# First block's mixers: mLSTM ended by pairs of heads, output projection begun with seven of eight blocks, keys' norm by logarithm and exponential

## The chip, the cores and the metric

One core of a Trainium2 chip runs the whole program. The metric is the device time in microseconds of one execution. The kernel before takes 3124.77 us, the median of three runs (3122.93 to 3128.39).

## The reference, cut to what matters

A sequence of 512 tokens of width 1024 goes through two blocks. The change lies in the first block, which computes

```python
u = x @ w_in                                   # four mixers side by side, 256 columns out of each
y = concat(ssd(u0), rwkv(u1), gla(u2), mlstm(u3))      # 512 x 1024
x = layer_norm(alpha * x + y @ w_out)          # the output projection
logits = x @ router_w + router_b               # top 4 of 32 experts
x = layer_norm(alpha * x + moe(x) + ...)
```

Two details of the mixers are touched. RWKV divides its keys by their norm, per head of 64 channels: `kk = kk / max(norm(kk), 1e-12)`. The mLSTM has four heads of 64 channels, each with its own scores (512 x 512, causal), its own denominator `max(|den|, exp(-m))` and, after the output gate `sigmoid(og)`, its own group norm with centring. So the heads are independent of each other to the very end, where the output projection sums over all 1024 channels of the four mixers.

## The kernel before, in words

**The first block's mixers** are `block1_mix`. Channels lie on partitions where it suits (tiles of 128 x 512 tokens) and tokens lie on partitions elsewhere (tiles of 128 tokens x 4 chunks x 256 channels). Inputs and weights are split into a rounded half and a rest (`split`, lines 437 and 438), and a product is three matmuls (lines 449 to 451 and 466 to 468). `fproj` makes 128 channels on partitions, `tproj` is a generator that makes 256 channels with tokens on partitions, one chunk of 128 tokens at each `next`.

**The order of the work** is set by the framework's scheduler: the code is traced once, each engine then takes, among the instructions that are ready, the one that stands first in the program, and the result is one fixed order for each engine and each DMA queue. Buffers come from tagged pools: a tag has so many slots, and a tile takes a slot when its first instruction is issued. PSUM has eight banks; in `block1_mix` they belong to the pools `ps` (2, taken by `psb`), `pi` (3, the RWKV solves) and `pp` (3, the projections). After `block1_mix` the pool `psum` takes all eight anew, from the bottom: tag `gu` four (over both banks of `ps` and two of `pi`), `tr` two, `py` two. A tile of a new pool waits for the old tiles that lay in its place, and for no others.

**RWKV's keys** (`rwkv_prep`, lines 841 to 904, once for each half j of 128 channels): the keys are scaled (850), squared on ScalarE (851), summed per head by a matmul with a block matrix (853), and then come `Sqrt` on ScalarE (854), a maximum with 1e-12 (855) and a reciprocal (856) on VectorE, and the product (857). Beside it the decay's running sum is made and three exponentials are taken of it (869, 871, 872). The product goes to 875 and to GpSimd (877); the chain runs on over 878 to 885, after which TensorE makes the bonus (888) and the transposes (893, 899).

**The mLSTM** (`mlstm`, lines 729 to 789) comes last. For each head h and each key chunk si it makes decay weights on VectorE (752), takes their exponential on ScalarE (754), masks the diagonal on GpSimd (755), makes the scores on TensorE (757) and multiplies on VectorE (758); then ten products with the values (763) and a copy out of PSUM to `nd` on ScalarE (765). Between the heads `next(gate)` puts one chunk of the output gate's projection `mog`, whose `tanh` goes to `og` (744). After the four heads the activation table for logarithm and exponential is loaded (768), the projection's pools are closed, `out_begin` opens the tiles `mix` (the 1024 mixed channels, split) and `wo` (the split output weights) over the place of the closed pools, and the end follows for all four heads at once on 128 x 1024 elements: denominator (773 to 777), quotient (779), gate (781) and `post_norm` (566 to 572, with `fast_rsqrt`, lines 1083 to 1085). Then the pieces of `finish` of SSD, GLA and RWKV transpose their two blocks of 128 channels into `mix` (580, 583 to 587), the eight pieces of `w_out` are loaded and split (`out_piece`: 802, 804, 805), and the mLSTM's own two blocks are transposed. `fin` holds the four mixers' pieces in the order SSD, GLA, RWKV, mLSTM.

**The output projection** is in `block1_ffn`: for each of four token chunks t and two halves n of the columns it takes one bank `gu` and adds 8 blocks x 3 matmuls (`mm3`, lines 1148 to 1150), 192 in all. Then come the residual (1283), the layer norm (`row_norm`), the transposes (1297), the router (1301), the top four and the tables for the experts. The first expert starts with the gather of its rows (1428) and their transposes (1230). Then 32 experts run, one after the other, on weights that are streamed through a ring of buffers (1204) and split on ScalarE and VectorE (1213, 1214).

Of the kernel before, what the change touches and what calls it, by code (L numbers as in the profile page):

```python
# [8 lines left out]
F32 = mybir.dt.float32  # L9
# [364 lines left out]
def block1_mix(k, es_mix):  # L374
# [4 lines left out]
    with ExitStack() as es:  # L379
# [18 lines left out]
        def P(name, j=0):  # L398
            return colp[:, CP[name][0] + j:CP[name][0] + j + 1]
# [155 lines left out]
        def post_norm(y, nh, eps, center, gname, mi, between=None, fast=False):  # L555


            n = 256 // nh
            yv = y.rearrange("p c (h d) -> p (c h) d", h=nh)
            m = NCH * nh  # L560
            sq = wt([128, NCH, 256], "pn_sq")
# [14 lines left out]
            def finish(mix):  # L576
                for j in range(2):
# [4 lines left out]
                    if gname:  # L582
                        ACT.activation(mh, p, AF.Copy, scale=P(gname, j))
                        V.scalar_tensor_tensor(ml, p, P(gname, j), mh.bitcast(F32), op0=OP.mult, op1=OP.subtract)
# [144 lines left out]
        def mlstm():  # L729
# [16 lines left out]
            Wt = {}  # L746
            for h in range(4):
                j, r = h // 2, slice(64 * (h % 2), 64 * (h % 2) + 64)
                for si in range(NCH):
                    n = S - 128 * si  # L750
                    w = wt([128, n], "ml_w")
                    V.tensor_scalar(w, Gb[h][:, 128 * si:], cols[:, si, 64 + h:65 + h], 0.0,
                                    op0=OP.subtract, op1=OP.max)
                    ACT.activation(w, w, AF.Exp, scale=-1.0)
                    G.tensor_mul(w[:, :128], w[:, :128], C("incl"))
                    p = psb([128, n])
                    PE.matmul(p, kq[j][r, 128 * si:128 * si + 128], q[j][r, 128 * si:], start=True, stop=True)
                    V.scalar_tensor_tensor(w, w, 0.125, p, op0=OP.mult, op1=OP.mult)
                    Wt[si] = w
                p = psb([128, NCH, 65])  # L760
                for ti in range(NCH):
                    for si in range(ti + 1):
                        PE.matmul(p[:, ti], Wt[si][:, 128 * (ti - si):128 * (ti - si) + 128],
                                  mv[:, si, h], start=si == 0, stop=si == ti)
# [6 lines left out]
            den = wt([128, NCH, 4], "ml_den")  # L771
            dn = nd[:, :, :, 64]
            V.tensor_scalar(den, dn, -1.0, None, op0=OP.mult)
            V.tensor_max(den, den, dn)
            V.tensor_max(den, den, em)
            V.reciprocal(den, den)
            V.tensor_scalar(den, den, 0.5, None, op0=OP.mult)
            hh = wt([128, NCH, 256], "ml_h")
            V.tensor_mul(hh.rearrange("p c (h d) -> p c h d", h=4), nd[:, :, :, :64],
                         den[:, :, :, None].to_broadcast([128, NCH, 4, 64]))  # L780
            V.scalar_tensor_tensor(hh, og, 1.0, hh, op0=OP.add, op1=OP.mult)
            post_norm(hh, 4, 1e-5, True, "ml_g", 6, fast=True)
# [5 lines left out]
            fin[3](mix)  # L788

# [20 lines left out]
        def rwkv_prep():  # L810
# [34 lines left out]
            for j in range(2):  # L845
# [307 lines left out]
def block1_ffn(k, mix, wo, es_mix, b2):  # L1153
# [5 lines left out]
    with es:  # L1159
# [78 lines left out]
        with tile_pool(tc, name="w1", bufs=1) as w1:  # L1238
# [1312 lines left out]
```

## Time and profile before

| what | us |
|---|---|
| median of three runs | 3124.77 |
| the profiled execution's own time | 3125.81 |
| its span, from first to last instruction | 3124.0 |
| TensorE busy in the span | 2966.2 (95%) |
| VectorE, ScalarE, GpSimd busy | 2037.0, 1491.3, 537.4 |
| end of the mLSTM's last head (copy to `nd`) | 374.1 |
| first matmul of the output projection | 393.3 |
| last matmul of the output projection | 445.9 |
| first transposes of the first expert's rows | 477.2 |

Rows of the trace give the start in us from the span's beginning, the length, the engine, the line, the operation, the tiles written and read with their shapes, and in brackets the idle time before the instruction and what ended it. A merged row (x8) stands for so many instructions in succession. Engines are PE (TensorE), PEld (its weight loads), DVE (VectorE), ACT (ScalarE) and POOL (GpSimd). PEclk is the granted TensorE clock, 1.00 being 2.4 GHz and 0.50 being 1.2 GHz.

### The profile page before, as it was taken

To read this page: it belongs to the slowest core of one execution; us is meant where nothing else is said; L and a number is where in the kernel's file an instruction comes from. 1 tells how busy PE (TensorE), PEld (TensorE's weight loads), DVE (VectorE), ACT (ScalarE), POOL (GpSimd) and SP (SyncE) were. 2 spreads that over 40 slices of the span, in tenths; PEclk is the share of its full clock that TensorE was granted. 3 is DMA by queue.
4 is the path that set the end of the run, shared out by engine and by line. 5 is a ranking of instruction groups with operands and counts; after the bars stand their busy time and mean duration, and the time that the engine had idled before them with its cause. 6 is when DMAs were issued, how large, how long until landed. Compare 5 with 4: busy or idle time off the path is not lost. (4 is left out here: it accounts for less than half of the span.)

```text
span 3124.0 us, 41785 instructions
## 1 busy us (share of the span) xinstructions
PE 2966.2 (95%) x16609; PEld 2386.3 (76%) x16609; DVE 2037.0 (65%) x2862; ACT 1491.3 (48%) x1855; POOL 537.4 (17%) x444
## 2 busy tenths in 40 slices
PE   6899888999999999999999999999999899999997
PEld 4799765666666666666666888999999799888886
DVE  4755767988888888788887756654233846733324
ACT  4412346666666666666665633342222534432222
POOL 1210231101210000121002210320102501320104
PEclk8989989999999999999999989999999989999998
DMA  3201177989999999799996211122222211222221
GB/s 124 75 21 41 61 268 289 357 341 366 366 358 359 361 359 353 290 388 356 360 355 229 73 67 43 55 82 95 95 82 82 93 45 55 82 95 95 95 90 52
DMA packets 106263, 581.87 MB, mean 186 GB/s; under 512 B 13080, under 2 KB 13736, under 8 KB 56048
## 3 DMA queue, kind: packets, MB, share of 16 engines
q1 hardware_dynamic: 95120, 542.17, 44.9%
q0 software_dynamic: 10752, 36.47, 4.8%
q8 instruction: 132, 2.16, 0.3%
q10 hardware_dynamic: 192, 0.52, 0.1%
q14 instruction: 67, 0.55, 0.1%
HBM read 560.17 MB, written 18.94 MB: 185 GB/s over the span
## 5 line engine op out<-in xcount | busy, mean ns | idle before, releaser
L1214 DVE TENSOR_TENSOR wl<-w,wh 128x2048 fp32r<-128x2048 f32 (+1 forms) x367 | 800.8, 2197 | 125.7 <-ACT wh L1213 121.4
L1213 ACT ACTIVATE wh<-w 128x2048 fp32r<-128x2048 f32 (+1 forms) x375 | 668.3, 1810 | 51.4 <-PE gu L1150 34.9
L1816 PE MATMUL gu<-hh,w 128*128 128x264 f32 (+3 forms) x1336 | 419.0, 314 | 10.0 <-ACT hh L2518 10.0
L1817 PE MATMUL gu<-hl,w 128*128 128x264 f32 (+3 forms) x1336 | 415.6, 311 | 3.9 <-DVE hl L2520 3.8
L1818 PE MATMUL gu<-hh,w 128*128 128x264 f32 (+3 forms) x1336 | 413.5, 310 | 0.8 <-DVE w L1142 0.8
L1142 DVE TENSOR_TENSOR w<-w 128x1024 fp32r<-128x1024 f32 (+1 forms) x190 | 237.5, 1250 | 249.2 <-ACT w L1141 248.7
L1148 PE MATMUL gu<-wh,xT 128*96 128x512 f32 x896 | 371.9, 415 | 0.0
L1149 PE MATMUL gu<-wl,xT 128*96 128x512 f32 x896 | 359.4, 401 | 7.4 <-DVE wl L1214 7.2
L1150 PE MATMUL gu<-wh,xT 128*96 128x512 f32 x896 | 351.4, 392 | 0.0
L1141 ACT ACTIVATE w<-w 128x1024 fp32r<-128x1024 f32 (+1 forms) x194 | 201.3, 1038 | 297.7 <-PE gu L2338 89.6
L1816 PEld LDWEIGHTS gu<-hh,w 128*128 128x128 f32 x1336 | 260.0, 195 | 22.4 <-ACT hh L2518 11.6
L1817 PEld LDWEIGHTS gu<-hl,w 128*128 128x128 f32 x1336 | 260.0, 195 | 16.1 <-DVE hl L2520 5.0
L1818 PEld LDWEIGHTS gu<-hh,w 128*128 128x128 f32 x1336 | 260.5, 195 | 11.2 <-DVE w L1142 1.3
L1149 PE MATMUL py<-wl,hT 128*96 128x512 f32 x512 | 211.7, 413 | 1.8 <-DVE wl L1214 0.4
L1149 PEld LDWEIGHTS gu<-wl,xT 128*96 128x96 f32 x896 | 144.1, 161 | 87.1 <-DVE wl L1214 23.2
L1148 PE MATMUL py<-wh,hT 128*96 128x512 f32 x512 | 208.8, 408 | 1.4 <-ACT wh L1213 1.4
L1150 PE MATMUL py<-wh,hT 128*96 128x512 f32 x512 | 202.8, 399 | 0.0
L1148 PEld LDWEIGHTS gu<-wh,xT 128*96 128x96 f32 x896 | 144.4, 161 | 67.3 <-issue 7.4
L1150 PEld LDWEIGHTS gu<-wh,xT 128*96 128x96 f32 x896 | 145.4, 162 | 58.5
L2324 POOL TENSOR_TENSOR al<-fs,ah 128x528 fp32r<-128x528 f32 (+1 forms) x44 | 77.7, 1767 | 595.0 <-ACT ah L2323 595.0
L1428 POOL DMA_INDIRECT xg<-x_d,ix x32 | 72.8, 2275 | 505.5 <-DVE dx L1421 439.4
L1481 POOL DMA_INDIRECT h_d<-y,dx x31 | 60.6, 1955 | 526.2 <-ACT y L1480 496.6
(714 smaller groups left out, 6133.4 us busy)
## 6 DMA issues: line engine op xcount, KB each, us to landing
w<-in_wgu SPq DMA_DIRECT2D x256, 1024.0 KB, 8.4
w<-in_wdn SPq DMA_DIRECT2D x127, 1024.0 KB, 8.3
w<-in_w SPq DMA_DIRECT2D x88, 512.0 KB, 4.2
w<-in_w2f SPq DMA_DIRECT2D x43, 512.0 KB, 4.2
w<-in_w22a SPq DMA_DIRECT2D x32, 512.0 KB, 4.1
w<-in_w1f SPq DMA_DIRECT2D x18, 512.0 KB, 3.3
w<-in_w2o SPq DMA_DIRECT2D x16, 512.0 KB, 4.2
w<-in_w22b SPq DMA_DIRECT2D x16, 384.0 KB, 3.9
```

The source lines that it names most:

```text
L1141: nc.scalar.activation(h, w, AF.Copy)
L1142: (eng or nc.vector).tensor_sub(l, w, h.bitcast(F32))
L1148: PE.matmul(out, a[0], b[0], start=start, stop=False)
L1149: PE.matmul(out, a[0], b[1], start=False, stop=False)
L1150: PE.matmul(out, a[1], b[0], start=False, stop=stop)
L1213: ACT.activation(h[:, j], w[:, j], AF.Copy)
L1214: (early or V).tensor_sub(l[:, j], w[:, j], h[:, j].bitcast(F32))
L1428: gathers.append(G.indirect_dma_start(out=xg, out_offset=None, in_=x1_d, in_offset=bass.IndirectOffsetOnAxis(ap=ix[:, :1], axis=0)))
L1816: PE.matmul(p, w[0][:, kk], x[0][:, kk, c], start=kk == ks[0], stop=False)
L1817: PE.matmul(p, w[0][:, kk], x[1][:, kk, c], start=False, stop=False)
L1818: PE.matmul(p, w[1][:, kk], x[0][:, kk, c], start=False, stop=kk == ks[-1])
L2324: G.tensor_sub(a[1], ss[f], a[0].bitcast(F32))
```

## The change

Three things change, all in the first block.

1. **mLSTM.** The heads' loop becomes `heads(j)` for the pair 2j and 2j + 1, and the end becomes `end(j)` on that pair's 128 channels. The program order is now: heads 0 and 1 with the whole of the gate's projection, the table load, `out_begin`, `end(0)`, the blocks of SSD, GLA and RWKV, the eight pieces of `w_out`, the first pair's block, and only then heads 2 and 3, `end(1)` and the second pair's block. `post_norm` gets the arguments `j0` and `nb` for one block instead of two.
2. **Output projection.** Before the loop over chunks, four banks are begun (t = 0 and 1, n = 0 and 1) with the first seven blocks of `mix`, 21 matmuls each; the loop then adds the eighth block to these and does chunks 2 and 3 as before. The eighth block is the second pair of heads.
3. **Keys' norm.** The maximum is now taken of the sum of squares, straight from PSUM, with 1e-24; then `Ln` and `Exp` with scale -0.5 follow on ScalarE. Square root and reciprocal are gone.

```diff
-            Wt = {}
-            for h in range(4):
-                j, r = h // 2, slice(64 * (h % 2), 64 * (h % 2) + 64)
-                for si in range(NCH):
...
-                ACT.activation(nd[:, :, h], p, AF.Copy)
-                next(gate)
+            def heads(j):
+                for h in range(2 * j, 2 * j + 2):
+                    r = slice(64 * (h % 2), 64 * (h % 2) + 64)
+                    Wt = {}
+                    for si in range(NCH):
...
+                    ACT.activation(nd[:, :, h], p, AF.Copy)
+                    if j == 0:
+                        for _ in range(2):
+                            next(gate, None)
+
+            hh = wt([128, NCH, 256], "ml_h").rearrange("p c d -> p (c d)")
+            den = wt([128, NCH, 4], "ml_den")
+
+            def end(j):
+                hs_ = slice(2 * j, 2 * j + 2)
+                dj = den[:, :, hs_]
+                dn = nd[:, :, hs_, 64]
+                V.tensor_scalar(dj, dn, -1.0, None, op0=OP.mult)
+                V.tensor_max(dj, dj, dn)
+                V.tensor_max(dj, dj, em[:, :, hs_])
+                V.reciprocal(dj, dj)
+                V.tensor_scalar(dj, dj, 0.5, None, op0=OP.mult)
+                y = hh[:, 512 * j:512 * j + 512].rearrange("p (c d) -> p c d", c=NCH)
+                V.tensor_mul(y.rearrange("p c (h d) -> p c h d", h=2), nd[:, :, hs_, :64],
+                             dj[:, :, :, None].to_broadcast([128, NCH, 2, 64]))
+                V.scalar_tensor_tensor(y, og[:, :, 128 * j:128 * j + 128], 1.0, y, op0=OP.add, op1=OP.mult)
+                post_norm(y, 2, 1e-5, True, "ml_g", 6 + j, fast=True, j0=j, nb=1)
+
+            heads(0)
+            for _ in gate:
+                pass
             with tc.issue_after(last[-1].ins):
                 ACT.preload_act_table_set(LN_EXP)
             es2.close()
             out_begin()
...
-            post_norm(hh, 4, 1e-5, True, "ml_g", 6, fast=True)
+            end(0)
             for f in fin[:3]:
                 f(mix)
             for n in range(2):
                 for i in range(4):
                     out_piece(n, i)
             fin[3](mix)
+            heads(1)
+            end(1)
+            fin[4](mix)
...
-                ACT.activation(sq, p, AF.Sqrt)
-                V.tensor_scalar(sq, sq, 1e-12, None, op0=OP.max)
-                V.reciprocal(sq, sq)
+                V.tensor_scalar(sq, p, 1e-24, None, op0=OP.max)
+                ACT.activation(sq, sq, AF.Ln)
+                ACT.activation(sq, sq, AF.Exp, scale=-0.5)
                 V.tensor_mul(kk, kk, sq)
...
+            begun = {}
+            def project(t, n, qs):
+                c = slice(128 * t, 128 * t + 128)
+                if (t, n) not in begun:
+                    begun[t, n] = bank("gu")
+                for q in qs:
+                    mm3(PE, begun[t, n], (mix[0][:, q, c], mix[1][:, q, c]), (wo[n][0][:, q], wo[n][1][:, q]), q == 0, q == 7)
+                return begun[t, n]
+            for n in range(2):
+                for t in range(2):
+                    project(t, n, range(7))
             for t in range(NCH):
                 c = slice(128 * t, 128 * t + 128)
                 for n in range(2):
-                    p = bank("gu")
-                    for q in range(8):
-                        mm3(PE, p, (mix[0][:, q, c], mix[1][:, q, c]), (wo[n][0][:, q], wo[n][1][:, q]), q == 0, q == 7)
+                    p = project(t, n, range(7 if t < 2 else 0, 8))
```

## Rows read from the trace of the kernel before

**Rows 1.** Windows by stage: length; busy PE, PEld, DVE, ACT, POOL; PEclk, DMA, GB/s
```profile
376.80:393.30 16.50, 5.22 (x24) 3.97 (x24) 15.92 (x19) 12.30 (x18) 0.33 (x1) 0.64 0.67 224
393.30:398.60 5.30, 5.26 (x13) 4.17 (x14) 0.00 (x0) 3.71 (x4) 5.30 (x3) 0.51 0.92 336
393.30:445.90 52.60, 51.97 (x240) 42.94 (x241) 31.58 (x64) 19.70 (x29) 15.01 (x18) 0.95 0.71 257
445.90:477.20 31.30, 10.86 (x69) 9.60 (x67) 26.43 (x62) 17.17 (x30) 17.22 (x13) 0.56 0.73 253
477.20:1700.00 1222.80, 1206.29 (x5339) 799.99 (x5340) 1023.18 (x933) 809.90 (x694) 141.21 (x68) 0.99 0.91 347
```

**Rows 2.** Waits of PE from 0 to 330 us: total, times, longest
```profile
PE ps L888 <- DVE mxd L885: 10.4, 2, 7.4
```

**Rows 3.** Timeline of ACT around the keys' norm, first half, then second
```profile
61.09 0.60 ACT L854 ACTIVATE rsq<-ps 128x512 f32<-128x512 f32 x1
61.70 1.28 ACT L869 ACT_TABLE_LOAD   x1
63.00 0.63 ACT L869 ACTIVATE rsig<-rsig 128x512 f32<-128x512 f32 x1
...
87.66 0.60 ACT L854 ACTIVATE rsq<-ps 128x512 f32<-128x512 f32 x1
```

**Rows 4.** Timeline of DVE around the keys' norm, first half, then second
```profile
62.18 3.35 DVE L856 RECIPROCAL rsq<-rsq 128x512 f32<-128x512 f32 x1
65.45 1.16 DVE L438 TENSOR_TENSOR wl<-w,wh 128x1024 fp32r<-128x1024 f32 x1
66.53 0.68 DVE L857 TENSOR_TENSOR rkk<-rkk,rsq 128x512 f32<-128x512 f32 x1
...
75.10 0.75 DVE L885 SCALAR_TENSOR_TENSOR mxd<-mxd,colp 128x512 f32<-128x512 f32 x1
...
92.72 0.69 DVE L857 TENSOR_TENSOR rkk<-rkk,rsq 128x512 f32<-128x512 f32 x1
```

**Rows 5.** Timeline of ACT in the first layer norm, between its Ln and Exp
```profile
409.07 1.28 ACT L1085 ACT_TABLE_LOAD   x1
```

**Rows 6.** Timeline of PE: products of head 1, then all of head 3
```profile
357.66 2.34 PE L763 MATMUL ps<-mv,ml_w 128*128 128x65 f32 x20
...
367.39 1.77 PE L757 MATMUL ps<-ml_q,ml_k 64*128 64x512 f32 x4
...
369.52 0.70 PE L757 MATMUL ps<-ml_q,ml_k 64*128 64x256 f32 x2
...
370.46 0.48 PE L757 MATMUL ps<-ml_q,ml_k 64*128 64x128 f32 x2
...
371.33 2.34 PE L763 MATMUL ps<-mv,ml_w 128*128 128x65 f32 x20
```

**Rows 7.** Timeline of ACT: last head's copy and the gate's last chunk
```profile
373.71 0.39 ACT L765 ACTIVATE ml_nd<-ps 128x260 f32<-128x260 f32 x1 [5.83 <-PE ps L763]
375.92 0.38 ACT L744 ACTIVATE ml_og<-pp 128x256 f32<-128x256 f32 x1 [1.82 <-PE pp L468]
```

**Rows 8.** Timeline of DVE: first and last full-width step after the gate
```profile
376.60 1.23 DVE L781 SCALAR_TENSOR_TENSOR ml_h<-ml_og,ml_h 128x1024 f32<-128x1024 f32 x1
...
387.25 1.22 DVE L572 TENSOR_TENSOR ml_h<-ml_h,pn_s 128x1024 f32<-128x1024 f32 x1
```

**Rows 9.** Timeline at the first experts: DVE's row, then PE's two
```profile
469.11 0.54 DVE L1408 TENSOR_TENSOR o<-fcst,Rm 128x384 bf16<-128x384 f32 x1
...
477.20 1.51 PE L1230 MATMUL tr<-fcst,xg 96*128 96x96 f32 x8 [8.21 <-DMA xg<-x_d,ix]
...
480.46 0.45 PE L1411 MATMUL tr<-aux,o 128*96 128x6 bf16 x4
```

**Rows 10.** Groups by form, 330 to 450 us: busy, mean ns, idle before
```profile
L804 ACT ACTIVATE wo<-wraw 128x1024 fp32r<-128x1024 f32 x8 | 8.0, 1047 | 0.0
L805 DVE TENSOR_TENSOR wo<-wraw,wo 128x1024 fp32r<-128x1024 f32 x4 | 4.8, 1222 | 0.5 <-ACT wo L804 0.5
```

More of the change, by code (lines that the diff above doesn't have):

```diff
@@ L553, in rows, with post_norm @@
             return out
-        def post_norm(y, nh, eps, center, gname, mi, between=None, fast=False):
-            n = 256 // nh
+        def post_norm(y, nh, eps, center, gname, mi, between=None, fast=False, j0=0, nb=2):
+            n = 128 * nb // nh
             yv = y.rearrange("p c (h d) -> p (c h) d", h=nh)
             m = NCH * nh
-            sq = wt([128, NCH, 256], "pn_sq")
+            sq = wt([128, NCH, 256], "pn_sq").rearrange("p c d -> p (c d)")[:, :NCH * 128 * nb].rearrange("p (c d) -> p c d", c=NCH)
             sqv = sq.rearrange("p c (h d) -> p (c h) d", h=nh)
@@ L576, in finish @@
             def finish(mix):
-                for j in range(2):
+                for j in range(nb):
                     p = psb([128, 512])
@@ L582, in finish @@
                     if gname:
-                        ACT.activation(mh, p, AF.Copy, scale=P(gname, j))
-                        V.scalar_tensor_tensor(ml, p, P(gname, j), mh.bitcast(F32), op0=OP.mult, op1=OP.subtract)
+                        ACT.activation(mh, p, AF.Copy, scale=P(gname, j0 + j))
+                        V.scalar_tensor_tensor(ml, p, P(gname, j0 + j), mh.bitcast(F32), op0=OP.mult, op1=OP.subtract)
                     else:
@@ L745, in mlstm @@
             next(gate)
-            Wt = {}
-            for h in range(4):
-                j, r = h // 2, slice(64 * (h % 2), 64 * (h % 2) + 64)
-                for si in range(NCH):
[L750 to L764, printed above, removed]
-                ACT.activation(nd[:, :, h], p, AF.Copy)
-                next(gate)
@@ new lines, in heads @@
+            def heads(j):
[3 more added lines that the diff above has]
+                    for si in range(NCH):
+                        n = S - 128 * si
+                        w = wt([128, n], "ml_w")
+                        V.tensor_scalar(w, Gb[h][:, 128 * si:], cols[:, si, 64 + h:65 + h], 0.0,
+                                        op0=OP.subtract, op1=OP.max)
+                        ACT.activation(w, w, AF.Exp, scale=-1.0)
+                        G.tensor_mul(w[:, :128], w[:, :128], C("incl"))
+                        p = psb([128, n])
+                        PE.matmul(p, kq[j][r, 128 * si:128 * si + 128], q[j][r, 128 * si:], start=True, stop=True)
+                        V.scalar_tensor_tensor(w, w, 0.125, p, op0=OP.mult, op1=OP.mult)
+                        Wt[si] = w
+                    p = psb([128, NCH, 65])
+                    for ti in range(NCH):
+                        for si in range(ti + 1):
+                            PE.matmul(p[:, ti], Wt[si][:, 128 * (ti - si):128 * (ti - si) + 128],
+                                      mv[:, si, h], start=si == 0, stop=si == ti)
+                    ACT.activation(nd[:, :, h], p, AF.Copy)
+                    if j == 0:
+                        for _ in range(2):
+                            next(gate, None)
@@ L770, in mlstm @@
             out_begin()
[L771 to L781, printed above, removed]
-            post_norm(hh, 4, 1e-5, True, "ml_g", 6, fast=True)
+            end(0)
             for f in fin[:3]:
```

## The prediction

> **What bounds the kernel now.** I read the windows by stage first. From the first expert's transposes on, TensorE is busy 1206.29 of 1222.8 us at full clock [rows 1], so what is won before 477.2 moves the rest by the same amount. The stage before it has the one large hole of TensorE: between the gate (376.8) and the projection (393.3) it works 5.22 of 16.5 us, VectorE 15.92. The hole is paid a second time: in the first 5.3 us of the projection the granted clock is 0.51, the lower level of 1.2 GHz, after TensorE had mostly stood still; 5.26 us of work at half clock is some 2.6 us lost. The projection lasts 52.6 us, and the 31.3 after it belong to layer norm, router and tables, with VectorE busy 26.43 of them. Second I asked for TensorE's waits before 330: it waits 10.4 us in two waits, 7.4 and 3.0, for the end of the keys' chain, line 885 [rows 2]. So the change works at two places that end a wait of TensorE, and the two gains add.
>
> **Keys' norm.** Removed: Sqrt 0.60 [rows 3] and the reciprocal, 3.35 on VectorE [rows 4], with the maximum between them. Added: the maximum on PSUM, Ln and Exp. An ACTIVATE of this shape takes 0.60 to 0.63 [rows 3]; the maximum on PSUM is bounded by 0 (beside a table load) and one VectorE operation, 0.7. Ln and Exp lie in tables that follow each other with a load of 1.28 between them in the layer norm [rows 5], and I count the same load here. Before, such a load stood between Sqrt and the decay's Exp [rows 3], off the keys' path; now one stands on that path, and the one for line 869 goes. From the sums' end at 61.09: Ln 0.63, load 1.28, Exp 0.63 make 63.6, and with up to 0.7 for the maximum 64.4. The product of line 857 stood at 66.53, after the reciprocal and a split of 1.16 that got in ahead of it [rows 4]. It moves 2.1 to 2.9 us forward; I take 2.4. In the second half, Sqrt starts at 87.66 and the product at 92.72; Ln, load and Exp give 90.2, or 90.9 with the maximum, so 1.8 to 2.5, and I take 2.4, the end nearer to the case with the maximum under a load. The chain behind the product (line 885 stood at 75.10) moves with it unless the decay's exponentials, now 0.65 later, end last. Sum -4.8; bounds 0 and -5.4. The waits of 7.4 and 3.0 can hold 2.4 each.
>
> The load at 61.70 lasts 1.28 and the Exp behind it starts at 63.00, 0.02 us after it [rows 3]: no further cost shows. The Trainium skill, "ScalarE: Activation LUTs", section "What ACT_TABLE_LOAD costs", puts a drain of 1.38 us beside the load at each switch; rows 3 and 5 do not show it behind the load.
>
> **First pair and gate.** Head 1's products end at 357.66 + 2.34 = 360.0 [rows 6]; the last chunk of the gate is copied at 375.92 [rows 7]. Of the 15.9 us between, heads 2 and 3 take TensorE for 2 x (2.34 + 1.77 + 0.70 + 0.48) = 10.6 [rows 6]. Without them the gate's rest is 5.3 us, so it is complete at about 365.7, 10.2 earlier.
>
> **end(0).** From the gate's step to the last full-width step of the norm it takes 376.60 to 388.47 now, 11.9 us [rows 8]. Half the width saves 0.6 of each such step; five of them make 3.1. So 8.8: the pair is ready at 365.7 + 8.8 = 374.5, its transposes at 375.1 (an estimate: two blocks with their copies took 388.47 to 393.3, 4.8, and the four transposes of one block are a quarter of its 2.4).
>
> **Second pair.** Banks of one tag seem to be handed out in program order, not by need: the tables' product of line 1411 ran at 480.46, though its input was ready at 469.65 and TensorE stood idle 8.21 us until the gather's transposes ran at 477.20 [rows 9]. If so, the scores of heads 2 and 3 cannot take a bank of `ps` before the first pair's block has, and start at 375.1, where they are nearly done today. A head takes 367.39 to 373.67, 6.3 us [rows 6]; two make 12.6. The copy to `nd` adds 0.4 [rows 7], and a piece of `wo` that gets in on ScalarE 1.05 [rows 10]. So the second pair is out at 389.1, where today all four heads are out at 374.1. end(1) takes 374.10 to 388.47 in today's width, 14.4 [rows 7, 8], less 3.6 for six steps at half width, less some 2 for the blocks of the other mixers, which VectorE copies in that stretch now and would have behind it: 8.8. With 2.4 for its block the eighth block of `mix` is complete at 400.3. Today the eighth is there at 393.3: it comes 7 us later, and the projection has 7/8 of its first two chunks, 84 of 192 matmuls or 23 us, to run before it.
>
> Moved with it: the loads of `w_out` now stand on SP ahead of heads 2 and 3, in a pool from which the four mixer tiles are still held, and the loads of the residual and the constants queue behind them; I cost them at nothing, because in the projection's 52.6 us VectorE needs nothing before the first residual. GpSimd, which has no work between 376.8 and 393.3 (0.33 us), masks heads 2 and 3 there. Without that cover a late load of x holds the first residual, not TensorE.
>
> **Forecast (A).** The first bank of the projection lies on a bank of `ps` that is free after head 3's copy, at 389.1. The projection then runs from 389.1 behind end(1), 52.6 us as now, to 441.7 instead of 445.9: -4.2. The hole does not vanish, it is filled by heads 2 and 3, which came out of the stretch before it. The 31.3 behind it stay. Sum -4.8 - 4.2 = -9.0, from the profiled execution's 3125.81 to 3116.8 (the median of the runs, 3124.77, is 1.04 below that execution; against the median it would be 3115.8).
>
> **Rivals.**
> B, the early start doesn't happen. `psum` is laid from the bottom over both banks of `ps`, and a bank waits for its old tiles. The second pair's block is the last taker of a `ps` bank; if it has the bank of the first `gu` tile, none of the 84 matmuls can start before its copy at 400.3. Then the projection starts 7.0 later, and the tail is 2 shorter, because VectorE's backlog (26.43 of 31.3 busy [rows 1]) is worked off earlier: +7.0 - 2 - 4.8 = +0.2, 3126.0. For it: the two banks alternate, and the last tile must have one of two; against it, which one can't be read from this trace.
> C, slower. The pieces of `wo` and the other mixers' copies stand in the program before heads 2 and 3 and go first on ScalarE and VectorE: 4 x 1.22 and 2 x 1.05 [rows 10] make 7.0 us in a pair that is bound by these two engines. The pair ends at 396, and the first bank is blocked as in B: +14.0 - 2 - 4.8 = +7.2, 3133.0. It decides from the point where the pair ends after 396.
> D, better. If banks go by need, heads 2 and 3 are not held back and run under the gate and end(0), and the seven blocks follow with no hole: the idle 16.5 - 5.22 = 11.3 and the half clock's 2.6 go, -13.9 - 4.8 = -18.7, 3107.1. Against it: the row of line 1411.
> E, the drain. At the two table switches that come onto the keys' path, an idle stretch as long as the load, some 1.4 us, would follow each load, and the gain there would be 2.0: 3119.6. Rows 3 and 5 speak against it. The Trainium skill, "ScalarE: Activation LUTs", section "What ACT_TABLE_LOAD costs", gives this drain.
>
> **How the numbers follow.** A 0.45, B 0.28, C 0.13, D 0.12, E 0.02. A tells itself from no change, because 0.2% of this kernel is 6.2 us, about what its measurement can resolve (the runs shown lie 5.5 apart). Faster by over 0.2%: most of A, D and E, less the part of A in which the keys give nothing: 0.50. Within: B and that part of A, 0.37. Slower: C, 0.13. The range goes from D, 3107, over A and B to 3128, which is B with half of the keys' gain lost; C and little else is left out. Positive cases hold most of the chance, so no second range is needed.
>
> **What would show it.** In the keys: no Sqrt and no reciprocal, a load between Ln and Exp, line 857 some 2.4 us earlier in each half, and TensorE's wait for line 885 at 5 to 6 us instead of 10.4. If that wait stays near 10, the chain ended elsewhere (GpSimd's line 877, the decay's exponentials), and the first term is wrong. In the mixers: the gate's last copy near 366, the last product of line 763 near 388.7, the eighth block near 400. The first matmul of line 1149 before that block says A, right behind it B, before 380 D. A second pair that ends after 396, with lines 804 and 805 between its steps, says C. The first gather's transposes (477.2 before) come at 468 in A, 477 in B, 484 in C, 458 in D. If they come at one of these and the time does not follow, then the experts' stage is not bound as I read it.

## The result and the profile after

The changed kernel takes 3146.92 us, the median of five runs (3136.28 to 3152.93), against 3124.77 before: a ratio of 1.0079, 95% interval 1.0059 to 1.0099; by the medians it is 22 us slower. The profiled execution has 3147.01, its span is 3145.2.

The stretches of the changed kernel by what TensorE does, where rows 1 showed those of before (length; busy PE, PEld, DVE, ACT, POOL; PEclk, DMA, GB/s): from the gate to the second pair, the second pair, the wait for its end, the projection, and from there to the first expert.

```profile
367.50:378.00 10.50, 5.44 (x30) 3.91 (x28) 8.79 (x15) 8.65 (x15) 0.00 (x0) 0.75 0.57 165
378.00:398.30 20.30, 18.86 (x56) 13.06 (x56) 7.74 (x12) 6.52 (x9) 11.26 (x5) 0.50 0.29 97
398.30:406.80 8.50, 0.73 (x4) 0.74 (x5) 5.69 (x13) 1.42 (x4) 1.67 (x8) 0.50 0.00 0
406.80:463.40 56.60, 54.02 (x243) 44.19 (x241) 29.92 (x54) 17.91 (x26) 3.48 (x6) 0.92 0.80 287
463.40:501.40 38.00, 12.61 (x69) 11.10 (x67) 28.13 (x73) 17.36 (x30) 17.12 (x13) 0.50 0.50 175
```

TensorE is nearly always busy in the second stretch, at 1.2 GHz; in the third it stands. The projection took 52.6 us and takes 56.6, and the way from its end to the first expert took 31.3 and takes 38.0 [rows 1].

TensorE's timeline of the changed kernel: the first other block, the first pair's block, the scores (759) and products (765) of heads 2 and 3, the last block (580), the first projection matmul (1167), the first expert's transposes (1249).

```profile
367.51 1.04 PE L580 MATMUL ps<-cst,ys 128*128 128x128 f32 x8
...
375.93 1.11 PE L580 MATMUL ps<-cst,ml_h 128*128 128x128 f32 x4 [0.56 <-DVE mix L587]
378.01 3.44 PE L759 MATMUL ps<-ml_q,ml_k 64*128 64x512 f32 x4 [0.96 <-DVE mix L587]
...
384.47 4.53 PE L765 MATMUL ps<-mv,ml_w 128*128 128x65 f32 x20 [0.16 <-DVE ml_w L760]
388.93 4.86 PE L759 MATMUL ps<-ml_q,ml_k 64*128 64x512 f32 x8
393.72 4.53 PE L765 MATMUL ps<-mv,ml_w 128*128 128x65 f32 x20
406.07 1.11 PE L580 MATMUL ps<-cst,ml_h 128*128 128x128 f32 x4 [7.82 <-DVE ml_h L572]
406.83 0.78 PE L1167 MATMUL gu<-wo,mix 128*128 128x512 f32 x1
...
501.39 1.51 PE L1249 MATMUL tr<-fcst,xg 96*128 96x96 f32 x8 [10.22 <-DMA xg<-x_d,ix]
```

Three things are to be seen. The products of a head take 4.53 where they took 2.34 [rows 6]. The projection does not start early: it comes right behind the last block's transposes, after 7.82 us in which TensorE stands. And the first expert comes at 501.39 instead of 477.20 [rows 9]; 24.2 us are lost by then, 21.2 in the span.

VectorE's timeline shows the residuals of chunk 0, one for each half of the columns, first of the kernel before, then of the changed one. The first of them came 8.2 us behind the first projection matmul (393.34) and now comes 21.6 behind it:

```profile
401.53 0.69 DVE L1283 SCALAR_TENSOR_TENSOR x<-x,gu 128x512 f32<-128x512 f32 x1 [8.24 <-PE gu L1150]
...
406.97 0.69 DVE L1283 SCALAR_TENSOR_TENSOR x<-x,gu 128x512 f32<-128x512 f32 x1 [0.49 <-PE gu L1150]
```

```profile
428.48 1.37 DVE L1314 SCALAR_TENSOR_TENSOR x<-x,gu 128x512 f32<-128x512 f32 x2 [8.14 <-PE gu L1169]
```

TensorE's waits up to 330 us, where rows 2 had 10.4 for the keys' chain (the wait of line 451 for line 438 was 0.5):

```profile
PE ps L907 <- DVE mxd L904: 7.4, 2, 4.7
...
PE pp L451 <- DVE wl L438: 4.5, 2, 4.0
```

### The profile page after: what moved, and what is told of

It is laid out like the page before. It is cut to its first block, busy times and chain, and to the rows that moved or that the text cites. A ratio compares the mean times of both kernels' runs of the same rounds, so it can differ in the third digit from the quotient of the medians.

```text
span 3145.2 us, 41803 instructions
## 1 busy us (share of the span) xinstructions
PE 2975.6 (95%) x16609; PEld 2392.6 (76%) x16609; DVE 2030.3 (65%) x2873; ACT 1496.5 (48%) x1862; POOL 540.8 (17%) x444
## 5 line engine op out<-in xcount | busy, mean ns | idle before, releaser
L1233 DVE TENSOR_TENSOR wl<-w,wh 128x2048 fp32r<-128x2048 f32 (+1 forms) x367 | 801.9, 2199 | 126.6 <-ACT wh L1232 122.5
```

Source lines behind the costliest of these rows:

```text
L1233: (early or V).tensor_sub(l[:, j], w[:, j], h[:, j].bitcast(F32))
```

## The experiments

The same code reaches the mLSTM's first scores at 326 to 344 us from one execution to the next (the last section shows why). So the stations stand in us after these first scores, 338.04 before and 341.04 in the changed kernel. Each entry is the row's time less that of the kernel's first scores row; the ratio is that of all its runs to runs of before on the same chip.

| kernel | last product ends | last block | projection starts | ends | first residual | first expert | ratio, 95% interval |
|---|---|---|---|---|---|---|---|
| before | 35.7 | 50.6 | 55.3 | 108.1 | 63.5 | 139.2 | |
| changed | 57.2 | 65.0 | 65.8 | 122.4 | 87.4 | 160.3 | 1.0079 (1.0059 to 1.0099) |
| keys_only | 36.9 | 51.9 | 54.7 | 107.5 | 62.5 | 139.6 | 1.0012 (0.9998 to 1.0025) |
| early_only | 35.6 | 50.6 | 55.3 | 107.2 | 77.8 | 148.4 | 1.0039 (1.0023 to 1.0055) |
| early_two | 35.4 | 50.8 | 55.5 | 107.5 | 68.0 | 139.6 | 0.9997 (0.9979 to 1.0014) |
| pairs_only | 57.8 | 65.7 | 68.4 | 125.4 | 76.8 | 154.2 | 1.0044 (1.0025 to 1.0062) |
| no_early | 57.8 | 65.7 | 66.4 | 122.5 | 74.3 | 151.0 | 1.0053 (1.0035 to 1.0071) |
| heads_first | 41.7 | 67.8 | 70.4 | 126.0 | 77.8 | 154.4 | 1.0038 (1.0017 to 1.0059) |
| n1_on_vector | 41.5 | 63.3 | 65.9 | 122.1 | 73.9 | 150.4 | 1.0030 (1.0010 to 1.0049) |
| other_banks | 56.3 | 64.1 | 64.8 | 120.8 | 72.7 | 149.3 | 1.0042 (1.0021 to 1.0063) |
| ends_first | 44.2 | 56.6 | 59.2 | 113.7 | 67.2 | 153.6 | 1.0043 (1.0021 to 1.0064) |
| filled | 52.0 | 60.4 | 63.1 | 118.8 | 70.6 | 146.9 | 1.0027 (1.0008 to 1.0046) |
| true_start | 54.1 | 62.9 | 35.7 | 110.0 | 66.9 | 151.5 | 1.0050 (1.0022 to 1.0079) |
| both | 53.8 | 62.2 | 34.6 | 108.7 | 66.4 | 150.9 | 1.0052 (1.0031 to 1.0073) |
| start_const_late | 54.0 | 62.8 | 35.7 | 112.8 | 66.9 | 149.9 | 1.0051 (1.0032 to 1.0071) |
| const_late | 35.5 | 50.8 | 55.6 | 111.6 | 63.1 | 143.7 | 0.9999 (0.9981 to 1.0017) |

Most of the last column follows one event. Chunk 0 is finished with its second residual. That one comes at 68.9 before, 88.1 in the changed kernel, 78.5 in early_only, 68.6 in early_two and 82.2 in pairs_only (in a merged row of two, at half its length), and from there to the first expert it is 69.9 to 72.2 us in all kernels down to filled, ends_first apart (79.9). So in these the experts' start goes with the projection's first finished chunk. In the kernels below filled that stretch is longer.

**The three parts alone.** Each was put into the kernel before, or taken out of the changed one.

```diff
keys_only:  before, with only
-                ACT.activation(sq, p, AF.Sqrt) ... V.reciprocal(sq, sq)
+                V.tensor_scalar(sq, p, 1e-24, None, op0=OP.max); Ln; Exp with scale -0.5
early_only: before, with only
+            for n in range(2):
+                for t in range(2):
+                    project(t, n, range(7))
pairs_only: the changed kernel without both of these
no_early:   the changed kernel without the second
```

> The kernel before with the keys' norm of the change and nothing else. Forecast's term: -4.8 us, the wait of TensorE for the keys' chain falls from 10.4 to 5 or 6. Rival, after reading the changed kernel: there the product of the keys' norm came 2.3 us sooner after the square than before, but the wait only fell to 7.4, other waits of the same stretch grew by 5.7, and the first scores of the mLSTM came at 341.0 instead of 338.0; by that the edit alone gives between -1 and +4 us.

> The kernel before with the projection begun with seven of eight blocks, and nothing else. Theory 'order': the new pool's banks are given only once the last tile of the old pool has begun, so the first matmul still stands right behind the last block's transposes (within 1.5 us of 393.3), and the first chunk's bank is complete some 60 matmuls, 14 us, later than before; VectorE's first residual comes at 412 to 416 instead of about 399, and the first expert's transposes 7 to 12 us after 477.2. Rival 'start': the projection begins before the last block is there, and the time stays or falls by up to 5 us.

> The changed kernel without the early projection and with the old keys' norm: only the mLSTM by pairs. Theory: heads 2 and 3, moved into the stretch in which TensorE otherwise stands, run at half clock with 9 to 11 us each instead of 6.3, and the last block comes 13 us later than before; the projection starts at 404 to 408 and the time is 8 to 14 us over before. Rival: the pairs are free and all of the loss is the projection's order; projection at 392 to 396, time within 3 us of before.

> The changed kernel without the early projection (pairs and new keys' norm stay). If the losses add: 8 to 14 us over before, and 8 to 14 under the changed kernel; the 38.2 us between the last projection matmul and the first expert's transposes fall back to 30 to 32. Rival: the tail stays at 38, because it is the late start and not the order of the projection that makes it long.

The parts nearly add up in the trace: the first expert comes 0.4, 9.2 and 15.0 us later with the keys, the early order and the pairs alone, 24.6 together; the changed kernel has 21.1. The pairs with the new keys' norm (no_early) come only 11.8 later, and 11.8 and 9.2 make 21.0. Of the 3.2 between the two kernels with pairs, 2.0 lie at the projection's start: in pairs_only its first matmul waits for the last block's copy out of PSUM, in no_early and in the changed kernel there is no such wait.

```profile
406.21 0.80 PE L1166 MATMUL gu<-wo,mix 128*128 128x512 f32 x1 [1.56 <-DVE mix L584]
```

The ratios add as well (0.12 + 0.39 + 0.44 = 0.95% against 0.79%, within the intervals).

The early order alone, TensorE and VectorE of early_only:

```profile
393.61 0.79 PE L1148 MATMUL gu<-wo,mix 128*128 128x512 f32 x1 [2.79 <-DVE mix L584]
...
416.13 1.37 DVE L1295 SCALAR_TENSOR_TENSOR x<-x,gu 128x512 f32<-128x512 f32 x2 [9.26 <-PE gu L1150]
...
486.69 1.51 PE L1230 MATMUL tr<-fcst,xg 96*128 96x96 f32 x8 [8.47 <-DMA xg<-x_d,ix]
```

The projection starts at the same place and ends 0.9 us sooner, and still the first expert is 9.2 us later, because the first residual comes 14.3 us later (77.8 against 63.5) and the whole of chunk 0 9.6 (78.5 against 68.9). What the theory called 'order' said of chunk 0 and of the first expert held, 'start' fell. Why the first matmul stands behind the last block is not shown here: it waits 2.79 us for the last block's copy (line 584), as it does in the kernel before, so its bank was not free. Only the changed kernel, where it has no such wait, tells the order from the bank. With the pairs alone the theory held: the heads took 11.0 and 9.3 us, the projection started at 406.21, and the first expert's 15.0 us are a little over what was expected. For no_early, the sum held: the first expert is 11.8 us over before and 9.3 under the changed kernel, and the tail, 122.5 to 151.0, is 28.5 us against 37.9, even less than the 30 to 32 expected; its rival fell.

The keys' edit alone on ScalarE, second half, and what came of it on VectorE and TensorE:

```profile
88.87 1.28 ACT L856 ACT_TABLE_LOAD   x1
90.17 0.63 ACT L856 ACTIVATE rsq<-rsq 128x512 f32<-128x512 f32 x1
90.82 1.28 ACT L857 ACT_TABLE_LOAD   x1
92.11 0.63 ACT L857 ACTIVATE rsq<-rsq 128x512 f32<-128x512 f32 x1
92.65 1.04 ACT L437 ACTIVATE wh<-w 128x1024 fp32r<-128x1024 f32 x1
...
97.90 2.06 DVE L438 TENSOR_TENSOR wl<-w,wh 128x1024 fp32r<-128x1024 f32 x1
...
100.02 0.49 PE L451 MATMUL pp<-xh,wl 128*128 128x512 f32 x1 [3.97 <-DVE wl L438]
```

In the first half the product of the keys' norm comes at 63.98 instead of 66.53, 2.6 us sooner. The end of its chain (line 885) comes only 1.3 sooner, at 73.76 instead of 75.10 [rows 4], because the split of 1.16 that had got in ahead of the product now stands behind it and lasts 2.06. In the second half ScalarE takes the decay's three exponentials ahead of Ln; the product comes at 92.78 as before (92.72 [rows 4]), although this half's squares are made 1.3 us sooner (83.07 instead of 84.41), and the split of the next weights slips behind, so that TensorE waits 3.97 us for its rest. The wait for the keys fell by 2.4 (10.4 to 8.0), and that for the splits (line 451) grew by 4.0 (0.5 to 4.5): the forecast's term fell, the rival (-1 to +4 us) held.

**Is it chunk 0?** early_two begins only chunk 0's two banks with seven blocks.

```diff
-                for t in range(2):
-                    project(t, n, range(7))
+                project(0, n, range(7))
...
-                    p = project(t, n, range(7 if t < 2 else 0, 8))
+                    p = project(t, n, range(0 if t else 7, 8))
```

> The kernel before with only chunk 0's two banks begun with seven blocks (42 matmuls instead of 84). Theory: the loss of the early order comes from the late completion of chunk 0 as a whole; here chunk 0 is complete after 48 matmuls as in the kernel before, only its first half comes later, so the first expert's transposes come within 2 us of before (477.2, or 139.2 after the mLSTM's first scores) and the time is the same within 3 us. Rival: the first residual's delay is passed on as it is; 20 matmuls more before it are 4 to 5 us, and the transposes come 4 to 5 us later.

The first half of chunk 0 comes 4.5 us later, the whole chunk does not (68.6 against 68.9), and the first expert is where it was (139.6), the time too: the theory held. The price of the early order is the finish of the first chunk as a whole.

**Where the pairs lose 13 to 15 us.** Three kernels from pairs_only: heads 2 and 3 put first in the program; the blocks' transposes in the idle pool `pi`; and the first of these with GpSimd's pieces of `w_out` on VectorE.

```diff
heads_first:
             es2.close()
             out_begin()
+            heads(1)
             end(0)
...
-            heads(1)
             end(1)
other_banks:
-                    p = psb([128, 512])
+                    p = pi.tile([128, 512], F32, name="pi", tag="pi")
n1_on_vector: heads_first, and
-            (G if n else V).tensor_sub(l, w, h.bitcast(F32))
+            V.tensor_sub(l, w, h.bitcast(F32))
```

> The pairs-only kernel with heads 2 and 3 put in the program ahead of the first pair's end, the other mixers' blocks and the pieces of w_out; gate early and ends by pairs stay. Theory: what the pairs cost is the place of heads 2 and 3, not the ends by pairs. The two heads run at 6 to 7 us each, the last product of line 763 ends at 374 to 378 instead of 393.3 (pairs only: 391.18 to 395.7), the projection starts at 390 to 396 and the time is within 4 us of before. Rival: the doubled small steps of the ends cost it; the projection starts after 400 as with the pairs alone, time 10 us or more over before.

> The pairs-only kernel with the blocks' transposes in the three idle banks of the pool pi, so that heads 2 and 3 need not wait in ps until the first pair's block has had its bank. Theory: the order of the banks holds the two heads back; without it their first scores come at 367 to 371 instead of about 376, the last product 5 to 10 us earlier than with the pairs alone and the time 4 to 10 us below 3139. Rival: the other mixers' copies and the pieces of w_out on ScalarE and VectorE hold them; the first scores come within 2 us of the pairs-only kernel and the time is within 3 us of it.

> The kernel with heads 2 and 3 first (heads_first), with the four pieces of w_out that GpSimd subtracted put on VectorE. There the small steps of the second pair's end took 2.00, 2.27 and 2.03 us instead of 0.17, and the quotient 2.78 instead of 0.69, from 392.7 to 402.1, while GpSimd worked on those pieces from 392.3 to 401.5. Theory: VectorE's steps are stretched while GpSimd runs; without GpSimd they take 0.17 to 0.7 again, VectorE gets 4.9 us more to do, and the last block's transposes come 2 to 5 us earlier relative to the mLSTM's first scores (67.8 there). Rival: the steps waited for something else; they stay at 2 us and the last block comes 5 us later.

Neither place nor bank alone was it. In heads_first the last product ends at 41.7 instead of 57.8, near the 36 to 40 of the theory (374 to 378 less 337.85), and yet the last block is 2.1 us later than with the pairs alone and the projection starts at 70.4, so the forecast of the time fell. Its VectorE and GpSimd show why:

```profile
392.66 2.00 DVE L780 TENSOR_TENSOR ml_den<-ml_den,ml_nd 128x8 f32<-128x8 f32 x1
394.69 2.27 DVE L781 TENSOR_TENSOR ml_den<-ml_den,ml_em 128x8 f32<-128x8 f32 x1
396.99 0.20 DVE L782 RECIPROCAL ml_den<-ml_den 128x8 f32<-128x8 f32 x1
397.23 2.03 DVE L783 TENSOR_SCALAR ml_den<-ml_den 128x8 f32<-128x8 f32 x1
399.30 2.78 DVE L785 TENSOR_TENSOR ml_h<-ml_nd,ml_den 128x512 f32<-128x512 f32 x1
...
392.28 9.25 POOL L823 TENSOR_TENSOR wo<-wraw,wo 128x1024 fp32r<-128x1024 f32 x4 [32.65 <-ACT wo L822]
```

The second pair's end has its first step at 385.29 and the next only at 392.66, ten us after its products, because six copies and three pieces of `w_out` stand ahead of it on VectorE, which waits for ScalarE between them (3.94 and 1.08 us); and then its small steps, but for the reciprocal, last 2 us each, while GpSimd subtracts. In n1_on_vector GpSimd has no such work, and the same steps read:

```profile
394.71 0.17 DVE L780 TENSOR_TENSOR ml_den<-ml_den,ml_nd 128x8 f32<-128x8 f32 x1
394.91 0.17 DVE L781 TENSOR_TENSOR ml_den<-ml_den,ml_em 128x8 f32<-128x8 f32 x1
395.11 0.20 DVE L782 RECIPROCAL ml_den<-ml_den 128x8 f32<-128x8 f32 x1
395.35 0.17 DVE L783 TENSOR_SCALAR ml_den<-ml_den 128x8 f32<-128x8 f32 x1
395.56 0.69 DVE L785 TENSOR_TENSOR ml_h<-ml_nd,ml_den 128x512 f32<-128x512 f32 x1
```

The last block comes 4.5 us sooner (63.3 against 67.8), though VectorE has 4.9 us more to do: the theory held. In other_banks head 2's first scores do come 9.7 us sooner (27.9 after the first scores against 37.6), but the next ones then wait 6.55 us for VectorE's line 760; the last product and the last block gain 1.5 and 1.6, and the ratio stays (1.0042 against 1.0044). The order of the banks was a wait in front of another one.

Two more, since the kind of wait was still open: the ends ahead of copies and pieces, and TensorE kept busy.

```diff
ends_first:
             end(0)
+            heads(1)
+            end(1)
             for f in fin[:3]:
                 f(mix)
...
             fin[3](mix)
-            heads(1)
-            end(1)
             fin[4](mix)
filled: pairs_only, and behind heads(1)
+            warm = pi.tile([128, 512], F32, name="pi", tag="pi")
+            for i in range(96):
+                PE.transpose(warm[:, 0:128], cst[:, CF["ident"][0]:CF["ident"][0] + 128], ident)
```

> The pairs-only kernel with the program's order end(0), heads 2 and 3, end(1), and only then the blocks of SSD, GLA and RWKV, the pieces of w_out and the mLSTM's two blocks. In every kernel with pairs so far the last block's transposes come 62 to 68 us after the mLSTM's first scores (50.6 before), whether heads 2 and 3 run early, late, at full or at half clock. Theory 'queue': what the pairs cost is that 12 to 13 us of copies and pieces of w_out stand on VectorE and ScalarE ahead of the second pair's end; without that the last block comes at 50 to 55 and the time is within 4 us of before. Rival 'path': heads 2 and 3 now stand wholly behind the gate's 24 matmuls, and with the doubled small steps this sets the last block; it stays at 58 or more and the time 6 us or more over before.

> The pairs-only kernel with 96 transposes of a constant into an idle bank, of the lowest rank, which TensorE takes while it would stand between the gate and the last block; their result is not used. Theory 'queue': heads 2 and 3 run at full clock and in 6 to 8 us each instead of 9.3 to 11.0, the last product comes 4 to 9 us earlier than 57.9 after the first scores, the last block as much earlier (65.7 there), and the time is 3 to 8 us below the pairs alone. Rival: the heads are set by VectorE and ScalarE and not by the clock; last product and block stay within 2 us.

Of the 15.1 us by which the pairs delay the last block, the program's order on VectorE and ScalarE makes 9.1 (65.7 to 56.6 in ends_first). That lies between the two theories. The remaining 6 us were not taken apart; heads 2 and 3 run near half clock here too (0.57 from 366 to 383 us). What the half clock costs is seen in filled. TensorE's stretch from the second pair's scores to its last product, first in pairs_only, then in filled:

```profile
375.50:395.70 20.20, 18.83 (x56) 13.04 (x56) 7.70 (x12) 6.41 (x8) 11.29 (x5) 0.50 0.27 91
```

```profile
377.30:392.50 15.20, 15.20 (x96) 11.13 (x96) 7.49 (x12) 6.19 (x8) 10.67 (x5) 1.00 0.36 119
```

With useless work in between, the clock stays at 2.4 GHz, the pair takes 15.2 us instead of 20.2, the last block comes 5.3 us sooner and the first expert 7.3: the theory held in the trace. The intervals of the two ratios overlap (1.0008 to 1.0046, 1.0025 to 1.0062), so the gain in time is not shown by itself, and no run has both edits, so it is not shown either that the 9.1 and the 5.3 add.

ends_first recovers much of the last block and not the time: the first expert stays at 153.6, because the way from the first residual takes 86 us instead of 76. In its trace the last of the bias constants' steps stands in VectorE's row after the projection, in the midst of chunk 2's norm (453.09 to 455.35), and VectorE's steps are long beside 12.56 us of GpSimd's work. What share each has was not separated. Taking GpSimd's early subtractions off that stretch in the kernel before did not help:

```diff
splits_on_vector (splits_one keeps G for i < 1): before, and
-                    return unit(src, early=(G if i < 3 else V if i < 5 else None) if e == 0 else None)
+                    return unit(src, early=(V if i < 5 else None) if e == 0 else None)
```

> The kernel before with GpSimd's eight early subtractions of the first expert's weights (449.2 to 461.7 us, in the tail of the projection) put on VectorE. In that stretch VectorE's steps of the norm and the top four are some 5 us longer than elsewhere (2.01 and 1.82 instead of 1.28, 1.07 and 1.25 instead of 0.2 to 0.3). Theory: VectorE is stretched while GpSimd runs, as in heads_first; without it the first expert's transposes come 1 to 5 us sooner after the mLSTM's first scores (139.2) and the time is 0 to 5 us below before. Rival: the eight subtractions, 5.4 us of VectorE, stand in the same chain; transposes 0 to 5 us later.

> The same with one of the three pieces left on GpSimd. Theory: between the two, transposes 1 to 4 us sooner than before. Rival: as before or later.

The first expert comes at 145.5 and 146.1 after the first scores instead of 139.2, the ratios are 1.0015 (0.9998 to 1.0032) and 1.0013 (0.9994 to 1.0031). But splits_one is not the step between that it was meant to be: in `expert_unit` the call for i = 0 returns before the argument is read, so `G if i < 1` never applies, and its trace has the same sixteen subtractions on VectorE and none on GpSimd. It is a second execution of splits_on_vector, and the station differs by 0.6 us between the two. The theory fell; the rival's direction held, its size (0 to 5 us) was passed. In splits_on_vector VectorE's steps are short again (1.28 and 0.21 where they took 2.01 and 1.07), so GpSimd did stretch them; but the subtractions now stand between the steps of the chain, and that costs more than being stretched.

**A start that is early.** true_start opens three of the four `gu` banks in the place of the closed pool `pp`, before heads 2 and 3 end, and begins there; `both` adds the transposes in `pi`; start_const_late moves the bias constants behind the four chunks, const_late does that to the kernel before.

```diff
true_start: pairs_only, and
             es2.close()
+            k.b2.psg = k.b2.es.enter_context(tile_pool(tc, name="psg", bufs=1, space=PSUM, side="right"))
...
+            for t, n in ((0, 0), (0, 1), (1, 0)):
+                p = begun[t, n] = k.b2.bank("gu")
+                for q in range(7):
+                    mm3(PE, p, ..., q == 0, False)
             end(1)
```

> The pairs-only kernel with three banks of the projection opened in the place of the closed projection pool, before heads 2 and 3 end, and begun there with seven of eight blocks, 63 matmuls, chunk 0 first. Theory: nothing but the late opening of the new pool kept the projection behind the last block. The first matmul comes at 376 to 386, before the last block; TensorE is busy over 14 of the 17 us from 376 to 393 and at full clock there after the first few us, so that a head takes less than 9 us; the projection ends 12 to 20 us earlier than with the pairs alone (462.9), and the time is between 3110 and 3128. Rival: the pieces of w_out or the seven blocks come too late; the first matmul comes after 396 and the time stays within 5 us of the pairs-only kernel.

> The true start and the transposes in the idle banks together. If both theories hold: the two heads and the 63 matmuls fill the stretch from 368 on, the projection ends 3 to 8 us earlier than in the true start alone, and the time is between 3105 and 3122, below before. Rival: VectorE, busy all through that stretch, sets the last block, and the two together give no more than the true start.

> The true start with the bias constants behind the four chunks. In the true start the projection ended 110 us after the mLSTM's first scores (108 before) although 63 of its 192 matmuls came before the last block, because TensorE then waited for banks that VectorE had not emptied. Theory: VectorE has become the bound there; without the constants in between the projection ends at 98 to 106 and the transposes 3 to 8 us earlier than the 151.5 of the true start. Rival: the constants only move into the tail; transposes at 150 to 155.

> The kernel before with the experts' bias constants (some 11 us of VectorE in the projection) put behind the four chunks. Theory: in the projection and the tail VectorE's order decides; the chunks' norms come sooner and the first expert's transposes 2 to 6 us sooner than 139.2 us after the mLSTM's first scores; time 0 to 6 us below before. Rival: the constants lie in idle time of VectorE and put late they stand in the tail instead; transposes 3 to 8 us later.

This start works. TensorE of true_start, with head 3 in the midst of the projection, and its stretches to the first expert:

```profile
362.35 0.78 PE L1173 MATMUL gu<-wo,mix 128*128 128x512 f32 x1
...
374.43 1.77 PE L759 MATMUL ps<-ml_q,ml_k 64*128 64x512 f32 x4
...
378.37 2.34 PE L765 MATMUL ps<-mv,ml_w 128*128 128x65 f32 x20
```

```profile
376.00:390.00 14.00, 14.00 (x71) 11.12 (x70) 7.90 (x17) 1.44 (x4) 5.22 (x9) 1.00 0.00 1
390.00:436.00 46.00, 39.29 (x176) 32.59 (x176) 28.28 (x64) 17.99 (x27) 4.90 (x6) 0.89 0.77 284
436.00:478.00 42.00, 11.64 (x70) 10.01 (x68) 30.84 (x64) 17.04 (x29) 15.95 (x13) 0.55 0.68 231
```

The hole ahead of the last block is gone, the clock is full from 376 to 390 us, head 3 takes 6.3 us, and the projection begins 32.7 us sooner than with the pairs alone and ends 15.4 sooner. The theory of the late pool held, its time did not: the first expert gains 2.7 us of it. `both` gives 0.6 more, nothing to speak of, as its rival said. Moving the constants changed that by 1.6 (start_const_late, whose projection ended at 112.8 and not at 98 to 106) and cost 4.5 in the kernel before (const_late, the rival there held). Rows of true_start, first of ScalarE and TensorE, then of VectorE and GpSimd, show where much of the rest went:

```profile
416.76 1.09 ACT L1324 ACTIVATE x1T<-tr 128x512 f32<-128x512 f32 x2 [7.52 <-DMA h_d<-x1T]
417.42 1.91 PE L1327 MATMUL py<-rw,x1T 128*128 128x32 f32 x8 [5.94 <-ACT x1T L1324]
```

```profile
428.70 4.60 DVE L1290 TENSOR_TENSOR w<-w,bias 32x2048 f32<-32x2048 f32 x2 [0.19 <-ACT bias L1285]
...
444.47 6.77 DVE L1340 TENSOR_SCALAR gt<-m 128x4 f32<-128x4 f32 x1
...
443.84 7.36 POOL L1239 TENSOR_TENSOR wl<-w,wh 128x512 fp32r<-128x512 f32 x6
```

First, two chunks now come 3.8 us apart (ScalarE's line 1314 at 404.27 and 408.09), and ScalarE's copies of chunk 1 for the router wait 7.52 us for a store of one of the two `x1T` tiles to memory; TensorE stands for 5.94 us of that and VectorE for 10.67. `both` and start_const_late have the same wait (7.41 and 7.55), the kernel before has none. No run took it away. Then the gain goes into the chain of norm, router, top four and gather on VectorE; the 6.77 is a step of 0.2 us that lasts until the last of six subtractions of GpSimd has ended. What share each has was not separated. No version here is faster than the kernel before beyond its interval.

## Why the prediction was wrong

**What bounds the kernel** held: the time is lost before the first expert, and nearly all of it is carried to the end (24.2 there, 3.0 of them already at the mLSTM's first scores; 21.2 in the span).

**Keys' norm**, -4.8: right for the product in the first half (2.6 for 2.4), wrong in the second, and the sum was nothing or a loss (1.0012). The step that failed is that the chain "moves with it": even in the first half only 1.3 of the 2.6 reached its end. I had named the decay's exponentials as what could end last and did not ask in which order ScalarE takes them, nor what stood behind the norm on VectorE.

**Gate and hold** held. The gate's last copy came 26.7 us after the first scores (37.9 before), 11.2 sooner for a forecast of 10.2; heads 2 and 3 started at 37.0, forecast 37.1 (375.1 - 338.04). But other_banks shows that the named cause of the hold was one of two.

**Second pair**, 6.3 us a head: wrong. They took 11.0 and 9.3 (378.01 to 389.0 and 388.93 to 398.25), as the rows of a head came from a stretch at full clock and were used for one whose granted clock was 0.64, and 0.51 right behind it, before [rows 1]. With the clock held up (filled) the two still took 15.2, not 12.6, so the clock is 5.0 of the error and not all of it.

**end(1)** took 7.4 from the copy (398.68) to the last block (406.07); the forecast had 8.8.

**"The projection then runs from 389.1 behind end(1)"** failed, and with it the forecast A. The bank was free, as A had it: the projection's first matmul ran at 406.83, before the last block's copy at 407.22, so its bank was not that block's; the other bank of `ps`, which held head 3's products, was copied out at 398.68. But the matmul stood behind the last block's transposes in TensorE's order. That the new pool opens only after the old one is the reading that fits, and true_start shows that a pool opened earlier starts early; it puts the banks in another place too, so the two were not separated. The sentence ahead of the prediction, that a tile of a new pool waits for the old tiles in its place "and for no others", is thus not enough to tell when its first instruction runs. So B came true in effect, from another cause; its own cause, the blocked bank, is there in the kernel before, early_only and pairs_only (2.79, 2.79 and 1.56 us). C came true in its start: the second pair was out 57.6 us after the first scores, where C had 58 (396 - 338.04), though only in part by its cause, as filled shows.

**What was missing** in the sum and in every rival is the price of the order itself. I let 84 matmuls go first and kept "the 31.3 behind it", although the layer norm waits for chunk 0. B and C even gave the tail back 2 us; it grew by 6.7. The order is worth 9.2 us at the first expert (early_only). Between C's +7.2 and the measured execution's +21.2 lie 14.0; the 9.2 and the keys' 4.8 that did not come are as much, and the 12.0 that C gave the pairs lies near what they cost (11.8 with the new keys' norm, 15.0 without).

## What to carry to other kernels

An early start that rearranges a loop has to be priced once as if it didn't start early: ask which consumer waits for the first finished output, and when that now comes. Work that is moved into a hole of TensorE does not keep the duration it had in a dense stretch; price it at both levels of the clock (here 15.2 and 20.2 us for the pair). And where several pieces of work share VectorE, moving one in the program moves what stands behind it: read the queue, not only the step.

## What the runs showed of the hardware

A step of VectorE can be stretched by GpSimd: 0.17 to 2.0 us in heads_first, 0.2 to 6.77 in true_start, and back to 0.17 when GpSimd had nothing to do (n1_on_vector). The reciprocal between them stayed at 0.20 in heads_first. The Trainium skill, "SBUF — State Buffer", section "SBUF: two separate sides", says that the two engines share a pair of ports which one holds for a whole instruction while the other waits. The 2 us agree with GpSimd's 2.3 us an instruction (9.25 for 4). The 6.77 do not agree with one instruction (7.36 for 6): that step was let in only behind the sixth.

TensorE's clock can fall in a stretch in which TensorE never stands. The windows 200 to 225 us of the kernel before and of early_two, where both have the same code (RWKV's solves and GLA's scores); in the 30 us ahead of it TensorE is busy 30.00 us at 1.00 in both:

```profile
200.00:225.00 25.00, 25.00 (x125) 23.15 (x124) 5.57 (x12) 1.59 (x5) 2.90 (x5) 0.58 0.00 1
```

```profile
200.00:225.00 25.00, 24.49 (x197) 22.91 (x198) 8.01 (x20) 3.04 (x8) 8.38 (x14) 1.00 0.13 43
```

Busy 25.00 of 25 us at 0.58, and 197 instead of 125 matmuls at 1.00. Up to this stretch the same rows come 1.6 us later in early_two than in the kernel before, behind it 10.4 sooner: this stretch alone makes 12 us, and sets the first scores at 338.04 or at 327.67. So single executions can lie over 10 us apart by it; over all runs of the kernel before the fastest (3107.63) has a mean clock of 0.972 and the slowest (3134.47) of 0.961. Why some executions keep the clock was not settled.
